# Transposing attention weights: a float32 transpose on TensorE with the split in PSUM, against a float16 split with a transpose by DMA

## The chip, the cores and the metric

The kernel runs on one NeuronCore of a Trainium2 chip. The metric is device time in microseconds, the median of several executions. TensorE, VectorE, ScalarE, GpSimd and SyncE each run their own stream of instructions in order and wait for each other by semaphores. In the rows below they are PE, DVE, ACT, POOL and SP; PEld is TensorE's row of weight loads, which overlap its matmuls. SPq, ACTq are the queues of the engines that issue DMAs.

## What is computed

One inference step of a decoder layer: a prompt of 2048 tokens and eight samples of one token, model width 1024, all in float32. The change lies in the prompt's windowed attention. It is done for mixer A in three dilation branches (window and stride (128,1), (512,4), (2048,16), eight heads of 64) and for mixer B (window 128, eight query and two key heads, sinks). All four are the same banded attention in blocks of 128 queries:

```python
s = jnp.einsum('nbqhgd,nbkhd->nbhgqk', qb, kk, preferred_element_type=jnp.float32) * scale
s = jnp.where(valid[None, :, None, None], s, NEG)
lse = jax.nn.logsumexp(s, axis=-1)
p = jnp.exp(s - lse[..., None])
o = jnp.einsum('nbhgqk,nbkhd->nbqhgd', p.astype(vv.dtype), vv)
```

A block of queries sees its own block of keys and the one before it. Behind the attention come the output projection, cross-attention to 256 memory tokens and a gated feed-forward part with a short convolution.

## The kernel before

Float32 accuracy comes out of split operands: a large product is three matmuls of a high and a low part (`wh`, `wl` of the weights, `h`, `l` of the activations), split by ScalarE (L110, the high part) and VectorE or GpSimd (L120, the rest).

Phase 1 runs the input projection (`gemm_tile`, L667, 24 matmuls of 128x256 for a tile of 128 tokens and 256 columns) over the groups of 512 tokens and the column sets of `ORDER`. It writes q, k and v to DRAM. As soon as a group has its columns, attention jobs are queued: kinds d1, d4 and d16 for the branches of mixer A, b for mixer B, 16 jobs of each kind. Each job is 128 queries and eight heads, and is done as two *quads* of four heads, so there are 128 quads. A quad has one key half (d16, and the first block of the others) or two.

After each tile of the projection `filler` takes a few steps of the attention (`attn_step`, L623). Three steps make one turn, and a turn moves the pipeline by a quad:

- `stage_a` (L534): the scores on TensorE into the banks `se` and `so` (L548); VectorE adds the mask and takes the maximum of each row, one instruction per head (L556), and makes the bias from it (L559); ScalarE takes the exp of each head with its sum (L561). The unnormalised weights are in `sm`, float32, queries on partitions.
- `stage_b` (L565), a turn later: ScalarE copies `sm` to float16 (L569), VectorE subtracts that copy for the second float16 part (L570), both into `p2`; a DMA transpose issued by SyncE (L572) brings `p2` to `pT`, with keys on partitions.
- `stage_c` (L576): for each head and key half five matmuls (L585) with a transposed 128x128 block as the stationary operand, three with the high part and the three bfloat16 parts of the values, two with the low part. A copy (L592) moves the result out of bank `o`.

The queue `ready` (L616, L654) holds two quads between `stage_b` and `stage_c`, so the DMA has two turns. Queries and keys of a job are transposed by TensorE, four 128x128 blocks to a group, into one of two PSUM banks with tag `t` (`t_split` L469 and L473, `t_copy` L478 and L482), and split or copied from there. The buffers: `sm` 2, `p2` 2, `pT` 3, `ost` 5. At the start of the program some of these buffers serve as room for the first tiles of x (`at_start`).

The order in each engine's stream is not the order of the source alone: a scheduler moves instructions by its own timeline, so that pieces of `stage_a` to `stage_c` and transposes stand in the middle of a tile's matmuls. The turn as the source has it is

```python
        elif s == 1:
            nxt = None
            if pipe["b"]:
                jb, i, sm = pipe["b"]
                nxt = (jb, i, *stage_b(jb, i, sm))
```

Phase 2 (output projection, cross-attention, feed-forward) starts when all the attention is done; it uses lines L862 to L864 for its matmuls.

Of the kernel before, what the change touches and what calls it, by code (L numbers as in the profile page):

```python
# [8 lines left out]
F32 = mybir.dt.float32  # L9
F32R = mybir.dt.float32r  # L10
F16 = mybir.dt.float16
BF16 = mybir.dt.bfloat16
ACTF = mybir.ActivationFunctionType
ALU = mybir.AluOpType
# [7 lines left out]
NS = 8  # L22
# [13 lines left out]
def tile_layer(ctx: ExitStack, tc: tile.TileContext, I, C, O):  # L36
    nc = tc.nc
# [32 lines left out]
    act = nc.scalar.activation  # L70
    vec = nc.vector
# [17 lines left out]
    ident = const.tile([128, 128], F32, tag="ident", name="ident")  # L89
# [141 lines left out]
        vec.tensor_scalar(out=out, in0=ss, scalar1=scale, scalar2=EPS, op0=ALU.mult, op1=ALU.add)  # L231
        pl.tensor_tensor(out=out, in0=out, in1=mhalf[:rows, :n], op=ALU.pow)

    # ------------------------------------------------------------------ phase 1
    p1 = ExitStack()
    p1a = ExitStack()
    psA = ctx.enter_context(tc.tile_pool(name="psA", bufs=1, space=PSUM))
# [4 lines left out]
    def bank(tag, bufs, dt=F32):  # L242
        return ps.tile([128, 512], dt, tag=tag, name=tag, bufs=bufs)
# [6 lines left out]
    sinkb = sbR.tile([128, 8], F32, tag="sinkb", name="sinkb")  # L250

    def at_start(tag, bufs):
        """a tile in the place of one that the attention uses later."""
        return sbR.tile([128, 1024], F32, tag=tag, name="x0", bufs=bufs)

    def load_x(src, rows=128, t=None):
# [27 lines left out]
    def xprep(key, nxt=None):  # L284
        rows = NS if key == "s" else 128
        x = x_tiles.pop(key)

        def norm():
            ss = sbL.tile([128, 1], F32, tag="ss", name="ss", bufs=3)
            junk = at_start("sm", 2) if key in range(4) else sbL.tile([128, 1024], F32, tag="xr", name="junk")  # L290
            act(out=junk[:rows], in_=x[:rows], func=ACTF.Square, accum_out=ss[:rows])
            r = sbL.tile([128, 1], F32, tag="r", name="r", bufs=18)
            rms_r(r[:rows], ss[:rows], 1.0 / D, 1, rows)
            rows_r[key] = r

        if key == "s":
            norm()
            pt = bank("t", 2)
            for k in range(8):
                nc.tensor.transpose(pt[:, k * NS:(k + 1) * NS], x[:NS, k * 128:(k + 1) * 128], ident[:NS, :NS])  # L300
            vec.tensor_copy(out=xsT, in_=pt[:, 0:64].rearrange("p (k n) -> p k n", k=8))
            xg = sbL.tile([128, 8, NS], F32, tag="xgs", name="xgs")
            pl.tensor_tensor(out=xg, in0=xsT, in1=vecs[:, 0:8].unsqueeze(2).to_broadcast([128, 8, NS]), op=ALU.mult)
            la = sbL.tile([128, 8, 40], F32R, tag="la", name="la")
            lb = sbL.tile([128, 8, NS], F32R, tag="lb", name="lb")
            pl.memset(la.bitcast(F32), 0.0)
            vec.tensor_copy(out=la[:, :, 0:NS], in_=xg)
            vec.tensor_copy(out=lb, in_=xg)
            lo_of(la[:, :, 32:32 + NS], xg, la[:, :, 0:NS])
            xT[key] = (la, lb)  # L310
            return
        if key != 0:
            norm()
        if key in (1, 2, 3):
            xr = at_start(*(("p2", 2), ("p2", 2), ("pT", 3))[key - 1]).rearrange("p (k t) -> p k t", k=8)
        else:
            xr = sbL.tile([128, 8, 128], F32, tag="xr", name="xr")
        for hf in range(2):
            pt = bank("t", 2)
            for k in range(4):  # L320
                kk = hf * 4 + k
                nc.tensor.transpose(pt[:, k * 128:(k + 1) * 128], x[:, kk * 128:(kk + 1) * 128], ident)
            act(out=xr[:, hf * 4:hf * 4 + 4, :], in_=pt.rearrange("p (k t) -> p k t", k=4), func=ACTF.Copy)
        if key == 0:
            norm()
        xT[key] = xmul(xr, x)
        dma(out=xt_d.rearrange("(k p) t -> p k t", p=128)[:, :, key * 128:(key + 1) * 128], in_=xr)
        rope_tab(key)
        if nxt is not None:
            x_tiles[nxt[0]] = load_x(nxt[1], NS if nxt[0] == "s" else 128)  # L330
# [35 lines left out]
        vec.tensor_tensor(out=out, in0=t1[:rows, :n], in1=t2[:rows, :n], op=ALU.add)  # L366

    def v_split(src, nh):
        """three bf16 parts of the values, exact to float32."""
        v3 = sbL.tile([128, 4, 3, 64], BF16, tag="vs", name="vs", bufs=2)[:, 0:nh]  # L370
        rs = sbL.tile([128, 256], F32, tag="vr", name="vr", bufs=1)[:, 0:nh * 64].rearrange("p (h d) -> p h d", d=64)
        s = src.rearrange("p (h d) -> p h d", d=64)
        pl.tensor_copy(out=v3[:, :, 0, :], in_=s)
        pl.tensor_tensor(out=rs, in0=s, in1=v3[:, :, 0, :], op=ALU.subtract)
        pl.tensor_copy(out=v3[:, :, 1, :], in_=rs)
        pl.tensor_tensor(out=v3[:, :, 2, :], in0=rs, in1=v3[:, :, 1, :], op=ALU.subtract)
        return v3
# [45 lines left out]
            dma(out=s_bk[:, 127, :], in_=z3[:, 0:128])  # L423
            dma(out=s_bv[:, 127, :], in_=z3[:, 128:256])

    # ---- windowed attention, four heads at a time
    class Job:
        def __init__(self, kind, t, c=0):
            self.kind, self.t, self.c = kind, t, c
# [55 lines left out]
    def job_prep(job):  # L485
# [9 lines left out]
        else:  # L495
# [20 lines left out]
            if job.kind == "d4" and job.t > 0:  # L516
                t_split([job.kp[:, 128 * j:128 * j + 128] for j in range(4)], rh[:, 0], rl[:, 0])
                vprev["d4"] = job.vp3
        # halves: list of (slot, v3) in key order
        v3 = job.v3  # L520
        first = job.kind == "d16" or job.t == 0
        if first:
# [11 lines left out]
    def stage_a(job, i):  # L534
# [5 lines left out]
        for ps_i, (a, b) in enumerate(passes):  # L540
            q_ = job.qh if a == 0 else job.ql
            k_ = job.kh if b == 0 else job.kl
            for u in range(2):
                p = 2 * i + u
                pk = 0 if job.kind == "b" else p
                for e in range(2):
                    r = slice(64 * e, 64 * e + 64)
                    mm(S[e][:, u * n:(u + 1) * n], q_[r, p, :], k_[r, s0:s0 + nh, pk, :],  # L548
                       start=(ps_i == 0 and u == 0), stop=(ps_i == len(passes) - 1), skip_group_check=True)
        sm = sbR.tile([128, 4, 256], F32, tag="sm", name="sm", bufs=2)  # L550
        mx = sbR.tile([128, 4], F32, tag="mx", name="mx", bufs=2)
        for u in range(2):
            for e in range(2):
# [9 lines left out]
        return sm  # L563

    def stage_b(job, i, sm):  # L565
        """the weights in two float16 parts, transposed by the DMA."""
        n = 128 * len(job.slots)
        p2 = sbR.tile([128, 2, 4, n], F16, tag="p2", name="p2", bufs=2)
        act(out=p2[:, 0], in_=sm[:, :, 0:n], func=ACTF.Copy)  # L569
        vec.tensor_tensor(out=p2[:, 1], in0=sm[:, :, 0:n], in1=p2[:, 0], op=ALU.subtract)  # L570
        pT = sbR.tile([128, 16, 128], F16, tag="pT", name="pT", bufs=3)[:, 0:n // 16]
        nc.sync.dma_start_transpose(out=pT, in_=p2.rearrange("p g x k -> p (g x k)"))  # L572
        v = pT.rearrange("p (g x h) t -> p g h x t", g=2, x=4)
        return v[:, 0], v[:, 1]

    def stage_c(job, i, ph, pl_):  # L576
        nh = len(job.slots)
# [35 lines left out]
    quads = deque()  # L613
    loaded = deque()
    pipe = {"b": None}
    ready = deque([None] * 2)  # L616
    sub = [0]
    d16_left = [16]

# [3 lines left out]
    def attn_step():  # L623
# [21 lines left out]
# [5 lines that stand above are left out]
            pipe["b"] = pipe["a"]  # L650
            pipe["n"] = nxt
        else:
            ready.append(pipe["n"])
            if len(ready) > 2:  # L654
                e = ready.popleft()
                if e:
                    stage_c(*e)
# [35 lines left out]
    MEM = []  # L693

    def mem_prep(t):
        """a tile of memory tokens, where the keys of the dilated branches have been."""
        if t == 0:
            while any(jb.kind != "b" for jb in [*jobs, *loaded, *(q[0] for q in quads)]):
                filler(1)
# [77 lines left out]
                    jobs.append(Job("b", 4 * b_next + t))  # L777
                b_next += 1

    # ------------------------------------------------------------------ phase 2  # L780
    p1a.close()
    p3 = ExitStack()
    sbA = p3.enter_context(tc.tile_pool(name="sb3a", bufs=1, reuse_waits="tile"))
# [16 lines left out]
    def xtile(nm):  # L800
        return sbA.tile([128, ST], F32, tag="xres", name=nm, bufs=9)[:, 0:NC]

    # state rows of the convolution, features on partitions
    srow = small("srow")[:, 0:384].rearrange("p (a c) -> p a c", a=3)
    sv = I["state_conv"][0].rearrange("n r (f p) -> (n r f) p", p=128)
    dma(out=srow[:, 0:2, :], in_=sv[0:256].rearrange("(a p) c -> p a c", p=128))
# [37 lines left out]
        return [(0, 256), (256, NC)] if has_s else [(0, 512)]  # L844

    def gemm_b(units, panels, pcs, evac, late=None, nm=2, spare=False):
        """units: list of (wh, wl, [panel indices]); evac(m, piece, psum)."""
        P = {}
        nu = len(units)
        for ui, (get, pidx) in enumerate(units):  # L850
# [25 lines left out]
                   lambda m, pi, a, b, p, mp=mp: evac(2 * mp + m, pi, a, b, p), spare=mp == 1 and len(pcs) == 2)  # L876

    class Norm:
        """mean of squares over the features, for each token."""

        def __init__(self, ncol, nlate=0):
            self.nlate, self.ncol, self.sqs, self.n = nlate, ncol, [], 0
# [76 lines left out]
                                     in1=gout[:rows, 512 * i:512 * i + 512], op0=ALU.mult, op1=ALU.mult)  # L959

    def merge(*ts, between=lambda: None):
        """the branches of mixer A weighted by their denominators, both mixers normalised."""
        wide = len(ts) > 1
        nb_ = 4 if wide else 2
        X = [merge_load(t) for t in ts]
# [35 lines left out]
            mo_t[t] = mo  # L1001
            between()

    # ---- decode-step attention over the caches
    def sample_softmax(S, nsl, nh, scale, sink, fix):
        """S: [128, NS, nsl, nh] raw scores -> normalised weights in place."""
        n = NS * nsl * nh
        Sf = S.rearrange("p n g h -> p (n g h)")
        M = sbA.tile([128, 256], F32, tag="sM", name="sM")
# [68 lines left out]
        return go  # L1078

    def pick(n, acc):  # L1080
        """the sum over the partitions, in row n."""
        h, l = (sbA.tile([128, ST], F32R, tag="sm2", name="ah", bufs=7)[:, 0:512] for _ in range(2))
        hi_of(h, acc, "a")
        lo_of(l, acc, h, "v")
        p = bankA("t")
        mm(p[:NS], sel[:, n, :], h, start=True, stop=False)
        mm(p[:NS], sel[:, n, :], l, start=False, stop=True)
        return p
# [60 lines left out]
        sample_steps.append(smp_out(n, "b"))  # L1149
    sample_steps.append(smp_fin)  # L1150

    # ---- cross attention of the samples
    SC = sbA.tile([128, NS, 2, 4], F32, tag="SC", name="SC")

    def xs_begin():
# [48 lines left out]
    cross_steps = [xs_begin] + [xs_score(n) for n in range(NS)] + \  # L1204
        [None] * 2 + soft_steps(SC, 2, 4, 0.0625, None, None) + [xs_out(n) for n in range(NS)] + [xs_fin]

    # ---- one chunk of 512 tokens
    def load_xres(c, hf):
        for m in range(4 * hf, 4 * hf + 4):
            t = xtile("xres")  # L1210
# [7 lines left out]
        return pn  # L1218

    def heads_T(c, oT):  # L1220
        """the merged heads of a chunk, features on partitions."""
        s_in = c == 2

        def one(k):
# [20 lines left out]
    def pre(c, oT, begin):  # L1245
# [20 lines left out]
        gemm_full(oT, pieces(s_in), ev_out)  # L1266
        del oT[:]

        # cross attention, one head after another
        q_t, kv_t, p_t = {}, {}, {}  # L1270
        R = [None]

# [258 lines left out]
        return fin  # L1531

    def fin_steps(c, fin):
        """the last norm and the output, half of the features after the other."""
        last = c == 3
        pts, ys = {}, {}

# [50 lines left out]
                store(i)  # L1588
        return go

    # keys and values of the memory tokens
    def mem_gemm(u, h, l):
        p = bankA("t")
        for kt in range(8):
# [141 lines left out]
```

## Time and profile before

| what | value |
|---|---|
| median of 3 runs | 3255.5 us (3251.39 to 3256.02) |
| span of the profiled execution | 3248.1 us |
| median over the profiled span | 7.4 us (the profiled execution's own time is not listed apart from the three runs) |
| busy share of TensorE, VectorE, ScalarE, GpSimd | 95%, 66%, 44%, 31% |
| attention products, first and last start | 136.6 and 994.9 us |

The span is the time from the first to the last instruction of the profiled execution. Busy time is the time in which an engine has an instruction; a matmul's end is modelled, so the next one often starts before it. An "idle before" with a releaser says who ended an engine's wait. Times in a window count from the span's start.

### The profile page before, as it was taken

The numbers are of one execution on the slowest core, as the hardware profiler recorded it, in microseconds if no ns is written. First come the engines' busy times: TensorE is split into PE (matmuls) and PEld (weight loads), VectorE is DVE, ScalarE is ACT, GpSimd is POOL, SyncE is SP. The second block draws the span as 40 slices with busy tenths as digits, with TensorE's granted clock in tenths as the row PEclk, the third lists the DMA queues.
The fourth block names the chain that finished last, engine by engine and source line by source line (L and its number), as shares of the span: only waits on it lengthen the run. The fifth ranks groups of instructions, "written<-read, shape, count | busy, mean of one in ns | idle before, by whom it ended". The sixth has DMA issues, their size and how long they took to land.

```text
span 3248.1 us, 58089 instructions
## 1 busy us (share of the span) xinstructions
PE 3101.2 (95%) x22280; PEld 2710.7 (83%) x22280; DVE 2140.0 (66%) x4292; ACT 1418.5 (44%) x2795; POOL 1018.7 (31%) x962
## 2 busy tenths in 40 slices
PE   8999989888888999998999999999999999999999
PEld 8888888788877887886887778898877778999998
DVE  7687777887886667664566766555676665654543
ACT  3556654666664444223344333444423333432322
POOL 2611613324343046332204424421454432110102
PEclk9999999999999999999999999999999999999999
DMA  7899998999897346653535545553465535222231
GB/s 210 246 255 241 263 241 231 259 241 216 198 232 225 114 159 212 200 196 130 196 112 174 183 159 175 172 188 111 158 239 213 189 123 185 72 86 92 91 93 66
DMA packets 621838, 580.14 MB, mean 179 GB/s; under 512 B 264141, under 2 KB 554105, under 8 KB 620433
## 3 DMA queue, kind: packets, MB, share of 16 engines
q1 hardware_dynamic: 616808, 572.21, 60.4%
q10 hardware_dynamic: 4608, 4.20, 0.4%
q8 instruction: 175, 2.87, 0.4%
q14 instruction: 103, 0.84, 0.1%
q0 software_dynamic: 144, 0.03, 0.0%
HBM read 457.55 MB, written 136.66 MB: 183 GB/s over the span
## 4 chain that ended last, share of the span: by engine, by line
PE 57%; DVE 5%; DMA 4%; POOL 4%; issue 3%; ACT 2%; SPq 1%; POOLq 0%; DVEq 0%; ACTq 0%
PE g L862 17%; PE g L863 17%; PE g L864 17%; PE s L1337 1%; PE g L1377 1%; DVE wl L120 1%; DMA pT<-p 1%; POOL mrg L990 1%; DMA mrg<-o_d 1%; DMA kx<-in_cache_mem_k_dram 1%; DMA vx<-in_cache_mem_v_dram 1%; POOL kx L1171 1%; ACT wh L110 0%; DMA wr<-in_w_mem_kv_dram 0%; PE t L1360 0%
## 5 line engine op out<-in xcount | busy, mean ns | idle before, releaser
L120 DVE TENSOR_TENSOR wl<-wr,wh 128x1024 fp32r<-128x1024 f32 (+1 forms) x406 | 534.1, 1316 | 369.6 <-ACT wh L110 368.4
L110 ACT ACTIVATE wh<-wr 128x1024 fp32r<-128x1024 f32 (+1 forms) x444 | 460.9, 1040 | 675.5 <-PE g L864 388.2
L862 PE MATMUL g<-h,wh 128*128 128x512 f32 (+2 forms) x2080 | 731.2, 352 | 1.4 <-DVE va L1495 0.7
L863 PE MATMUL g<-h,wl 128*128 128x512 f32 (+2 forms) x2080 | 729.9, 351 | 0.0
L864 PE MATMUL g<-h,wh 128*128 128x512 f32 (+2 forms) x2080 | 726.9, 350 | 0.0
L862 PEld LDWEIGHTS g<-h,wh 128*128 128x128 f32 x2080 | 391.5, 188 | 62.1 <-issue 2.2
L863 PEld LDWEIGHTS g<-h,wl 128*128 128x128 f32 x2080 | 391.5, 188 | 56.0 <-issue 1.7
L864 PEld LDWEIGHTS g<-h,wh 128*128 128x128 f32 x2080 | 391.4, 188 | 55.7
L672 PE MATMUL g<-wh,xh 128*128 128x256 f32 x1152 | 339.9, 295 | 1.9 <-ACT z L383 1.4
L674 PE MATMUL g<-wh,xl 128*128 128x256 f32 x1152 | 332.3, 288 | 0.3 <-DVE xl L120 0.3
L673 PE MATMUL g<-wl,xh 128*128 128x256 f32 x1152 | 331.0, 287 | 0.0
L862 PE MATMUL g<-act,wh 128*128 128x512 f32 (+2 forms) x880 | 311.0, 354 | 15.7 <-ACT act L110 8.0
L863 PE MATMUL g<-act,wl 128*128 128x512 f32 (+2 forms) x880 | 309.7, 352 | 0.0
L864 PE MATMUL g<-act,wh 128*128 128x512 f32 (+2 forms) x880 | 308.6, 351 | 0.0
L561 ACT ACTIVATE sm<-sm,ost 128x256 f32<-128x256 f32 (+1 forms) x512 | 234.7, 460 | 151.7 <-DVE ost L559 151.4
L892 POOL TENSOR_TENSOR sq<-sq 128x512 f32<-128x512 f32 (+1 forms) x83 | 126.2, 1520 | 484.6 <-ACT sq L887 451.8
L672 PEld LDWEIGHTS g<-wh,xh 128*128 128x128 f32 x1152 | 222.8, 193 | 7.2 <-ACT z L383 1.9
L674 PEld LDWEIGHTS g<-wh,xl 128*128 128x128 f32 x1152 | 222.0, 193 | 3.7 <-DVE xl L120 1.0
L673 PEld LDWEIGHTS g<-wl,xh 128*128 128x128 f32 x1152 | 222.7, 193 | 2.0
L862 PE MATMUL g<-oT,wh 128*128 128x512 f32 (+2 forms) x608 | 216.5, 357 | 3.1 <-ACT oT L110 3.1
L863 PE MATMUL g<-oT,wl 128*128 128x512 f32 (+2 forms) x608 | 215.8, 356 | 0.0
L864 PE MATMUL g<-oT,wh 128*128 128x512 f32 (+2 forms) x608 | 211.6, 355 | 0.0
(348 smaller groups left out, 6075.9 us busy)
## 6 DMA issues: line engine op xcount, KB each, us to landing
wr<-in_w_up_dram SPq DMA_DIRECT2D x176, 512.0 KB
wr<-in_w_down_dram SPq DMA_DIRECT2D x80, 512.0 KB
out_dram<-in_cache_a_k_dram SPq DMA_DIRECT2D x32, 1023.5 KB
out_dram<-in_cache_a_v_dram SPq DMA_DIRECT2D x32, 1023.5 KB
wr<-in_w_in_dram SPq DMA_DIRECT2D x60, 512.0 KB
v<-va_d SPq DMA_DIRECT2D x60, 384.0 KB
wr<-in_w_out_dram SPq DMA_DIRECT2D x32, 512.0 KB
wr<-in_w_xq_dram SPq DMA_DIRECT2D x32, 512.0 KB
```

What stands on the lines that cost most here:

```text
L110: act(out=out, in_=in_, func=ACTF.Copy)
L120: e.tensor_tensor(out=out, in0=in_, in1=hi.bitcast(F32), op=ALU.subtract)
L561: act(out=sm[:, x, 0:n], in_=sm[:, x, 0:n], func=ACTF.Exp, scale=0.125, bias=nb[:, x:x + 1], accum_out=job.ost[:, 520 + 4 * i + x:521 + 4 ...
L672: mm(p[:, 0:256], h[:, kt, :], wh[:, q, :], start=(kt == 0), stop=False)
L673: mm(p[:, 0:256], h[:, kt, :], wl[:, q, :], start=False, stop=False)
L674: mm(p[:, 0:256], l[:, kt, :], wh[:, q, :], start=False, stop=(kt == 7))
L862: mm(o, wh[:, q, c], pn[:, 0, a:b], start=st, stop=False)
L863: mm(o, wl[:, q, c], pn[:, 0, a:b], start=False, stop=False)
L864: mm(o, wh[:, q, c], pn[:, 1, a:b], start=False, stop=en)
L892: pl.tensor_tensor(out=acc[:, 0:self.ncol], in0=acc[:, 0:self.ncol], in1=sq[:, 0:self.ncol], op=ALU.add)
L990: pl.tensor_tensor(out=o, in0=o, in1=w[:, g, :].unsqueeze(2).to_broadcast([128, 8, 64]), op=ALU.mult)
L1171: pl.tensor_tensor(out=k[:, 0:1024], in0=k[:, 0:1024], in1=q[:, 0:1024], op=ALU.mult)
```

## The change

`stage_b` no longer splits in SBUF and no longer uses a DMA. For each key half it transposes the four float32 blocks of `sm` on TensorE into a bank `t` (a matmul against the identity, as `t_split` does it), copies the bank to float16 `pT` by ScalarE, and subtracts that copy from the bank by VectorE for the low part. `p2` and the DMA transpose are gone. `sm` has four buffers in place of two. `ready` holds one quad in place of two. `pT` has another shape, and the temporaries at the start that lay in `p2` lie in `sm`. Comments and docstrings are left out. Behind L575 the line numbers of the changed kernel are larger by two.

```diff
@@ xprep
-            junk = at_start("sm", 2) if key in range(4) else sbL.tile([128, 1024], F32, tag="xr", name="junk")
+            junk = at_start("sm", 4) if key in range(4) else sbL.tile([128, 1024], F32, tag="xr", name="junk")
...
-            xr = at_start(*(("p2", 2), ("p2", 2), ("pT", 3))[key - 1]).rearrange("p (k t) -> p k t", k=8)
+            xr = at_start(*(("sm", 4), ("sm", 4), ("pT", 3))[key - 1]).rearrange("p (k t) -> p k t", k=8)
@@ stage_a
-        sm = sbR.tile([128, 4, 256], F32, tag="sm", name="sm", bufs=2)
+        sm = sbR.tile([128, 4, 256], F32, tag="sm", name="sm", bufs=4)
@@ stage_b
-        n = 128 * len(job.slots)
-        p2 = sbR.tile([128, 2, 4, n], F16, tag="p2", name="p2", bufs=2)
-        act(out=p2[:, 0], in_=sm[:, :, 0:n], func=ACTF.Copy)
-        vec.tensor_tensor(out=p2[:, 1], in0=sm[:, :, 0:n], in1=p2[:, 0], op=ALU.subtract)
-        pT = sbR.tile([128, 16, 128], F16, tag="pT", name="pT", bufs=3)[:, 0:n // 16]
-        nc.sync.dma_start_transpose(out=pT, in_=p2.rearrange("p g x k -> p (g x k)"))
-        v = pT.rearrange("p (g x h) t -> p g h x t", g=2, x=4)
-        return v[:, 0], v[:, 1]
+        nh = len(job.slots)
+        pT = sbR.tile([128, 2, 2, 4, 128], F16, tag="pT", name="pT", bufs=3)
+        for hf in range(nh):
+            pt = bank("t", 2)
+            for x in range(4):
+                nc.tensor.transpose(pt[:, x * 128:(x + 1) * 128], sm[:, x, hf * 128:(hf + 1) * 128], ident)
+            v = pt.rearrange("p (x t) -> p x t", x=4)
+            act(out=pT[:, 0, hf], in_=v, func=ACTF.Copy)
+            vec.tensor_tensor(out=pT[:, 1, hf], in0=v, in1=pT[:, 0, hf], op=ALU.subtract)
+        return pT[:, 0], pT[:, 1]
@@
-    ready = deque([None] * 2)
+    ready = deque([None])
@@ attn_step
-            if len(ready) > 2:
+            if len(ready) > 1:
```

The scheduler places the new instructions. Three places in the streams show how. The first is TensorE in the kernel before, in the middle of the d16 jobs; L672 to L674 are the projection's matmuls, L585 the attention's products with a block of `pT` as weights.

```order
L672 MATMUL g_9515<-wh46_8572,xh_9047 128x256
L673 MATMUL g_9515<-wl46_8573,xh_9047 128x256
L674 MATMUL g_9515<-wh46_8572,xl_9048 128x256
L672 MATMUL g_9515<-wh46_8572,xh_9047 128x256
L585 LDWEIGHTS pT_8846
L585 MATMUL o_9055<-v3_8340,pT_8846 128x64
```

Here the products follow a run of the projection's matmuls, in the middle of a tile, and the first weight load is where TensorE stands if `pT` has not landed.

The second is the same engine in the changed kernel, again among the d16 jobs; L548 are the scores of the next quad, L572 the transposes of an earlier quad's weights, L674 to L676 the projection, L587 the products.

```order
L676 MATMUL g_10348<-wh47_9022,xl_9901 128x256
L548 MATMUL se_9829<-kf_9726,qf_9725 128x128
L548 MATMUL so_9830<-kf_9726,qf_9725 128x128
L548 MATMUL se_9829<-kf_9726,qf_9725 128x128
L548 MATMUL so_9830<-kf_9726,qf_9725 128x128
L572 MATMUL t_9847<-ident_81,sm_9714 128x128 x4
L587 LDWEIGHTS pT_9792
L587 MATMUL o_9908<-v3_9278,pT_9792 128x64
```

Between the scores of one quad and the products of another a group of four transposes now stands in TensorE's stream; the products use the `pT` of the group before it.

The third is TensorE in the changed kernel among the b jobs, where no projection is left between the steps; `ringb0` and `ringb1` are the two key halves.

```order
L548 MATMUL so_14249<-ringb0_13451,qh_14117 128x256
L572 MATMUL t_14177<-ident_81,sm_14024 128x128 x4
L572 MATMUL t_14184<-ident_81,sm_14024 128x128 x4
L548 MATMUL se_14248<-ringb1_13452,qh_14117 128x256
L548 MATMUL so_14249<-ringb1_13452,qh_14117 128x256
```

Both groups of a quad (`sm_14024`, into the two `t` banks) now stand inside the score matmuls of the next quad, with no matmul of a projection beside them.

## Rows read from the trace of the kernel before

**Rows 1.** The page, part 1: busy time, share of the span and instructions.

```profile
PE 3101.2 (95%) x22280; PEld 2710.7 (83%) x22280; DVE 2140.0 (66%) x4292; ACT 1418.5 (44%) x2795; POOL 1018.7 (31%) x962
```

**Rows 2.** Busy time by stretch: length, each engine, granted clock, DMA share.

```profile
core 0: us, PE busy (x) PEld busy (x) DVE busy (x) ACT busy (x) POOL busy (x), PEclk, DMA share, GB/s
100.00:300.00 200.00, 189.27 (x2128) 178.72 (x2127) 162.19 (x474) 117.45 (x310) 57.97 (x63) 0.99 0.99 252
850.00:1005.00 155.00, 126.30 (x1610) 113.17 (x1610) 122.81 (x348) 98.62 (x266) 67.09 (x44) 0.92 1.00 237
0.00:1005.00 1005.00, 895.20 (x10315) 828.52 (x10316) 779.25 (x2298) 580.49 (x1557) 345.97 (x324) 0.96 0.97 237
1005.00:3248.00 2243.00, 2205.97 (x11968) 1882.18 (x11966) 1360.72 (x1994) 838.00 (x1238) 672.68 (x638) 0.99 0.45 152
```

**Rows 3.** TensorE's waits, whole span: us in total, times, longest.

```profile
PE o L585 <- DMA pT<-p: 48.7, 37, 3.1
...
PE se L548 <- DVE mx L556: 14.4, 15, 2.5
...
PE t L473 <- DVE ql L120: 4.3, 4, 2.5
...
PEld L585 <- DMA pT<-p: 58.2, 44, 3.3
```

**Rows 4.** The products' line L585: duration min/median/max in ns, starts, forms.

```profile
L585 PE MATMUL o<-v,pT x3000: 192/193/261, 136.6 to 788.3; 128*128 128x64 bf16 x188
L585 PE MATMUL o<-v3b,pT x1240: 193/193/258, 790.0 to 994.9; 128*128 128x64 bf16 x178
```

**Rows 5.** Timeline of TensorE from 612.67 us: start, us, what.

```profile
612.67 0.28 PE L672 MATMUL g<-wh,xh 128*128 128x256 f32 x1
612.79 0.28 PE L673 MATMUL g<-wl,xh 128*128 128x256 f32 x1
612.91 0.28 PE L674 MATMUL g<-wh,xl 128*128 128x256 f32 x1
613.03 0.60 PE L482 MATMUL t<-ident,raw 128*128 128x128 f32 x4
613.38 0.36 PE L672 MATMUL g<-wh,xh 128*128 128x256 f32 x1
613.59 0.28 PE L673 MATMUL g<-wl,xh 128*128 128x256 f32 x1
```

**Rows 6.** The transposes of line L482: duration min/median/max in ns.

```profile
L482 PE MATMUL t<-ident,raw x160: 270/273/477, 116.3 to 647.0; 128*128 128x128 f32 x160
```

**Rows 7.** Groups by form, VectorE and ScalarE: busy us, mean ns, idle before.

```profile
L570 DVE TENSOR_TENSOR p<-sm,p 128x1024 f16<-128x1024 f32 x84 | 120.3, 1432 | 34.9 <-ACT p L569 34.6
L569 ACT ACTIVATE p<-sm 128x1024 f16<-128x1024 f32 x84 | 88.3, 1052 | 37.4 <-DMA pT<-p 36.8
L570 DVE TENSOR_TENSOR p<-sm,p 128x512 f16<-128x512 f32 x44 | 38.6, 878 | 24.1 <-ACT p L569 23.9
L120 DVE TENSOR_TENSOR ql<-t,qh 128x512 fp32r<-128x512 f32 x44 | 30.0, 681 | 2.1 <-ACT qh L110 2.1
L569 ACT ACTIVATE p<-sm 128x512 f16<-128x512 f32 x44 | 27.6, 627 | 22.5 <-DMA pT<-p 21.8
L110 ACT ACTIVATE qh<-t 128x512 fp32r<-128x512 f32 x44 | 25.9, 588 | 19.6 <-PE t L473 13.7 <-PE o L585 4.2 <-PE so L548 1.7
```

**Rows 8.** The DMA transposes in SP's queue: min/median/max in ns.

```profile
L572 SPq DMA_TRANSPOSE pT<-p x128: 1231/2986/7377, 129.0 to 986.7; - x128
```

**Rows 9.** Groups by form of `stage_a`: busy us, mean ns.

```profile
L561 ACT ACTIVATE sm<-sm,ost 128x256 f32<-128x256 f32 x336 | 166.4, 497 | 104.2 <-DVE ost L559 104.0
...
L561 ACT ACTIVATION_READ_ACCUMULATOR sm<-sm,ost 128x1 f32 x512 | 96.1, 188 | 0.0
...
L556 DVE CUSTOM_DVE_ANT_0 sm<-se,mask 128x256 f32<-128x256 f32 x168 | 64.7, 417 | 6.9 <-PE so L548 3.0 <-PE se L548 2.9
...
L559 DVE TENSOR_SCALAR ost<-mx 128x4 f32<-128x4 f32 x128 | 42.2, 330 | 0.8
```

**Rows 10.** Line L473, q/k transposes, by stretch: TensorE matmul, weight loads, clock.

```profile
100.00:300.00 200.00, 13.31 (x92) 10.03 (x92) 0.99 0.99 252
```

## The prediction

> **What bounds the kernel now.** I read the page's busy shares first: TensorE is busy for 95% of the span [rows 1], no other engine comes near. Then the stretches: the attention runs from about 100 to 1005 us, and behind it 2243 us follow in which TensorE is busy for 2206 [rows 2]. The change touches nothing behind 1005 us, so the question is what the first 1005 us become. There TensorE is busy for 895 us, VectorE for 779, ScalarE for 580, and the DMA engines are full (share 0.97); the mean granted clock is 0.96 [rows 2]. The clock has two levels, 1.2 and 2.4 GHz, so a mean of 0.96 is some 80 us at the lower one, which loses 40 us of matmul work.
>
> Third, who keeps TensorE waiting. One wait stands out: the attention's products (`stage_c`, L585) for the transposed weights `pT` that the DMA brings, 48.7 us in 37 waits on the matmul row, and 58.2 us in 44 on the row of weight loads, where the reader should look, because a wait shorter than a matmul's modelled tail shows only there [rows 3]. The other waits for VectorE are small: 14.4 us of the scores for the mask step, 4.3 us of the q/k transposes for the split that frees their bank [rows 3]. So the transposes by DMA cost TensorE 58 us directly, and more by the clock: in the stretch from 100 to 300 us, with little idle time, the clock is 0.99, in the last one, from 850 to 1005 us, with 29 us idle, it is 0.92 [rows 2].
>
> **The change part by part.** *Added on TensorE.* `stage_c` runs five products for each transposed 128x128 block, and there are 3000 + 1240 of them [rows 4], so there are 4240 / 5 = 848 blocks, in 212 groups of four, one group for each key half of each quad. The trace has the same operation already: four float32 transposes against `ident` (L482). Between the big matmul at 612.91 and the second one behind the group, at 613.59, lie 0.68 us; two matmuls without a group between them start 0.24 us apart. A group costs 0.44 us, changes of operand included [rows 5]. 212 x 0.44 = **+93 us**. They stand in TensorE's own stream, which is the path, so nothing hides them but a wait that they fill.
>
> *The duration of one transpose* is 273 ns [rows 6], two and a half times the 0.11 us spacing: they overlap in the pipeline. The Trainium skill (VectorE: DVE Perf Modes, the three transpose paths and the rules for kernel authors) advises TensorE for a 128x128 transpose where PSUM will do, at 390 ns against 1309 ns by DMA; by its figures, one block after the other, the 848 blocks would be an estimated gain of 848 x 0.919 = 779 us. The trace disagrees with the 390 (it has 273), and with the use of the difference: what counts is on whose time a transpose runs, and the DMA's ran beside TensorE and held it for 58 us. The sum stands on the 0.44 us.
>
> *Removed.* The wait for the DMA goes: **-58 us**, if nothing takes its place. Of the 40 us that the low clock takes, between nothing and all may come back. I take half, **-20 us**: the pT waits are the largest group in that part but not the only one, and new waits (below) keep some of it.
>
> *VectorE and ScalarE.* VectorE subtracts two 128x512 pieces out of PSUM in place of one 128x1024 out of SBUF. The before rows come to 120.3 + 38.6 = 158.9 us; 212 pieces at the 0.681 us of the q split are 144.4, so 14.5 us less. ScalarE: 88.3 + 27.6 = 115.9 us against 212 x 0.588 = 124.7, so 9 us more [rows 7]. At 779 and 580 busy of 1005 us neither sets the pace, so I cost both at nothing; if VectorE were the bound these would be a small gain.
>
> *SP's queue and the DMA engines.* 128 transposes leave SP's queue, at a median of 2.99 us each [rows 8]. Loads queued behind them go out earlier. TensorE hardly waits for those loads, so I count no gain.
>
> *Added waits.* Three things are new: a group of transposes waits for the exps of its quad (ScalarE), it waits for one of the two `t` banks, which the q/k transposes share and which VectorE's subtraction frees, and the products wait for that subtraction. From scores to the last exp a two-half quad takes 4 x 0.417 + 0.330 + 4 x (0.497 + 0.188) = 4.7 us [rows 9]; transposed, copied and subtracted takes 0.44 + 0.588 + 0.681 = 1.7 us more. In the stretches with big matmuls a turn of the pipeline has 17 to 30 of them (0.12 us each) beside the attention's own work, and most of both is covered. In the last stretch several turns have none, and scores, transposes and products follow each other directly, as the third piece of the order shows: what stands behind a waiting transpose there is everything, because TensorE's stream is in order. The bounds: three kinds at 4.3 us, as the q/k transposes wait now, is 13 us; three at 14.4 us, as the scores wait for VectorE now, is 43 us. I take the middle, **+28 us**. That `ready` holds one quad less costs nothing beyond this.
>
> *Sum.* 93 - 58 - 20 + 28 = **+43 us**. The profiled execution's span is 3248.1 us, so it becomes 3291; the median of the runs is 3255.5, 7.4 us over that span, so **3298.5 us**. With the bounds (clock -40 to 0, waits 13 to 43) the sum runs from +8 to +78 us, 3263.5 to 3333.5.
>
> **The rivals.** A difference of 0.2%, 6.5 us, is about what a measurement of this kernel can tell from no change.
>
> *Faster.* The 93 us fill waits. Besides the 58 and the whole 40, the 14.4 and 4.3 us of waiting for VectorE vanish, because more TensorE work stands between producer and consumer, and the new waits stay at nothing: 93 - 58 - 40 - 19 = -24 us, **3231.5**. For it: ScalarE's copy also stalled on `p` being read by the DMA, and this delayed exps. Against it: from 100 to 300 us the clock is 0.99 and TensorE is idle for 11 of 200 us [rows 2], so the groups there have nothing to fill. It turns faster where more than 100 of the 117 us are recovered. Chance 0.12.
>
> *Even.* All of the wait and of the clock's 40 us come back, and the new waits are a few us to the bound of 13: 93 - 98 + 5 = 0 us, **3255.5**. Chance 0.12.
>
> *The `t` banks become the bound.* A bank is held for 1.7 us by a group, of which 1.27 us are ScalarE and VectorE; there are two banks for the 212 new groups and for the q/k transposes. If in the 84 two-half quads (the wide form) [rows 7] the next user waits half of the 1.27 us, that is 84 x 0.63 = 53 us on top: +96, **3351.5**. For it: VectorE serves in order and the mask step of four 0.417 us pieces can stand ahead. Against it: the present waits on that ring are 4.3 us. Chance 0.14.
>
> *The clock falls more often.* If a group of transposes breaks up the run of matmuls as an idle gap does, the lower clock gets none of its 40 us back and takes half as much again: 93 - 58 + 20 + 28 = +83, **3338.5**. Against it: the q/k transposes are in the present stream too, 92 of them from 100 to 300 us [rows 10], where the clock is 0.99 [rows 2]. Chance 0.10. The Trainium skill (TensorE: Matmul & The Clock Gate, Part 4) says that transposes do not count as TensorE being busy for the clock; by that rule this rival gains weight. No row here separates the two.
>
> That the change does not do what it says can be left out: the order shows the 848 transposes on TensorE and none on SP's queue.
>
> **How the numbers follow.** The forecast has 0.52. Slower by over 0.2% are the forecast, the bank and the clock: 0.52 + 0.14 + 0.10 = 0.76. The even case gives 0.12 to within 0.2%, and the first rival 0.12 to faster. The forecast's own range is 3263 to 3334. To leave out no more than 2 in 10 it is widened to **3240 to 3350**: downwards over the even case and into the faster one, upwards over the clock's rival and up to the bank's price.
>
> **What would show it.** Right: 848 more matmuls on TensorE's row, spaced by 0.11 us in fours; no wait of the products for a DMA; the attention ends some 43 us later than 1005 us, and the stretch behind it keeps its 2243 us. The new waits appear on TensorE as transposes waiting for `sm` of ScalarE and products waiting for `pT` of VectorE, in sum 13 to 43 us, mostly behind 700 us; the clock up to the end of the attention is about 0.98. Wrong: groups much dearer or cheaper than 0.44 us, waits for the `t` bank of over 50 us, a clock at or under 0.96, or a part of the 2243 us that moves.

## The result, and the profile of the changed kernel

The change makes the kernel slower: 3290.8 us (median of four runs, 3286.08 to 3294.24) against 3254.2 us (four runs, 3251.39 to 3256.02), **+36.6 us**, a ratio of 1.0114 with a 95% interval of 1.0099 to 1.0129. The forecast was +43 us, 3298.5 us, and "slower" had 0.76. The profiled execution of the changed kernel has a span of 3292.5 us, 44.4 us over the one before and at the upper end of its runs, so its rows show about 8 us more than the medians do.

Part 1 of the page answers to [rows 1]: TensorE has 848 matmuls more and 96.7 us more of busy time, VectorE and ScalarE are where they were.

```profile
PE 3197.9 (97%) x23128; PEld 2801.3 (85%) x23128; DVE 2137.8 (65%) x4376; ACT 1427.3 (43%) x2879; POOL 979.1 (30%) x962
```

The windows of the changed kernel, columns as in [rows 2]. The attention ends 40 to 45 us later, so its windows reach to 1045 us.

```profile
100.00:300.00 200.00, 194.48 (x2137) 184.44 (x2136) 148.77 (x453) 108.64 (x294) 56.07 (x64) 0.99 0.65 202
850.00:1045.00 195.00, 177.67 (x2258) 160.38 (x2256) 149.90 (x480) 131.44 (x384) 61.81 (x50) 0.96 0.43 136
0.00:1045.00 1045.00, 989.56 (x11170) 918.09 (x11171) 780.40 (x2382) 588.74 (x1640) 309.75 (x324) 0.98 0.58 175
1045.00:3292.00 2247.00, 2208.37 (x11960) 1883.26 (x11958) 1357.43 (x1994) 838.59 (x1239) 669.35 (x638) 0.99 0.45 152
```

Read the third row against the third of [rows 2]. TensorE's busy time grows by 94.4 us (989.56 less 895.20), its idle time falls from 109.8 to 55.4 us, and the difference, 40 us, is what the stretch grew by. The DMA engines go from a share of 0.97 to 0.58, and the granted clock from 0.96 to 0.98. The fourth row shows that the 2243 us behind are 2247, and the 4 us between them are a matter of where the window's edge lies: the time is lost in the attention.

The products' line, as in [rows 4], tells the same without a window's edge: its last start moves from 994.9 to 1039.0 us, 44.1 us of the span's 44.4.

```profile
L587 PE MATMUL o<-v,pT x3000: 192/193/277, 128.4 to 832.2; 128*128 128x64 bf16 x188
L587 PE MATMUL o<-v3b,pT x1240: 191/193/261, 836.1 to 1039.0; 128*128 128x64 bf16 x178
```

TensorE's waits in the changed kernel, whole span, answering to [rows 3] (us in total, times, longest):

```profile
PE se L548 <- DVE mx L556: 6.1, 5, 2.5
PE t L572 <- DVE ql L120: 4.8, 5, 1.7
PE t L572 <- DVE pT L575: 4.6, 6, 1.6
PE o L587 <- ACT pT L574: 4.2, 7, 1.5
PE t L473 <- DVE pT L575: 3.5, 4, 1.5
...
PE t L572 <- ACT xr L323: 2.3, 2, 1.5
...
PE t L572 <- DVE ringb L120: 0.9, 2, 0.6
...
PE t L572 <- ACT sm L561: 0.7, 1, 0.7
```

No wait of the products for a DMA is left. In its place stand small ones, 21.0 us in all without the first row: 16.1 us are for a `t` bank that an earlier user holds (the rows of L572 that end with `ql`, `pT`, `xr` or `ringb`, and L473's for `pT`), 4.2 us are products that wait for ScalarE's copy, and only 0.7 us are transposes that wait for the exps (2.1 us on the row of weight loads). The scores' wait for the mask step fell from 14.4 to 6.1 us without being touched by the change.

The new instructions by form, and the transposes' line (duration min/median/max):

```profile
L575 DVE TENSOR_TENSOR pT<-t,pT 128x512 f16<-128x512 f32 x212 | 144.2, 684 | 43.3 <-ACT pT L574 42.3
L574 ACT ACTIVATE pT<-t 128x512 f16<-128x512 f32 x212 | 122.6, 590 | 122.9 <-PE t L572 121.7
```
```profile
L572 PE MATMUL t<-ident,sm x848: 270/273/477, 123.2 to 1036.4; 128*128 128x128 f32 x170
```

These match the prediction's 212 groups, 144.4 us, 124.7 us and 273 ns. Two groups in the timeline, start and length first: four transposes behind scores at 641.79 with the next matmul at 642.29, and four between two products.

```profile
641.79 0.66 PE L572 MATMUL t<-ident,sm 128*128 128x128 f32 x4
642.29 0.25 PE L587 MATMUL o<-v,pT 128*128 128x64 bf16 x3
...
300.80 0.40 PE L587 MATMUL o<-v,pT 128*128 128x64 bf16 x8
301.03 0.64 PE L572 MATMUL t<-ident,sm 128*128 128x128 f32 x4
301.50 0.22 PE L587 MATMUL o<-v,pT 128*128 128x64 bf16 x2
```

Products start 0.03 us apart, so the last of the eight starts at 301.00, and the next behind the group 0.50 us later: this group adds 0.47 us.

### The profile page after: what moved, and what is told of

Its sections match the earlier page's. It is cut to its first block, busy times and chain, and to the rows that moved or that the text cites. A ratio compares the mean times of both kernels' runs of the same rounds, so it can differ in the third digit from the quotient of the medians.

```text
span 3292.5 us, 59690 instructions
## 1 busy us (share of the span) xinstructions
PE 3197.9 (97%) x23128; PEld 2801.3 (85%) x23128; DVE 2137.8 (65%) x4376; ACT 1427.3 (43%) x2879; POOL 979.1 (30%) x962
## 4 chain that ended last, share of the span: by engine, by line
PE 59%; DVE 3%; POOL 2%; DMA 2%; issue 2%; ACT 1%; SPq 0%; POOLq 0%; DVEq 0%; ACTq 0%
PE g L864 18%; PE g L865 18%; PE g L866 18%; PE s L1339 1%; PE g L1379 1%; DVE wl L120 1%; POOL mrg L992 0%; DMA mrg<-o_d 0%; PE t L1362 0%; DMA vx<-in_cache_mem_v_dram 0%; PE t L1543 0%; PE t L1230 0%; POOL vx L1185 0%; DVE cv L1462 0%; PE t L903 0%
## 5 line engine op out<-in xcount | busy, mean ns | idle before, releaser
L674 PE MATMUL g<-wh,xh 128*128 128x256 f32 x1152 | 337.2, 293 | 2.2 <-DVE xh L114 1.6
L676 PE MATMUL g<-wh,xl 128*128 128x256 f32 x1152 | 333.7, 290 | 0.5 <-DVE xl L120 0.5
L674 PEld LDWEIGHTS g<-wh,xh 128*128 128x128 f32 x1152 | 220.8, 192 | 5.9 <-issue 1.7
L676 PEld LDWEIGHTS g<-wh,xl 128*128 128x128 f32 x1152 | 220.6, 191 | 2.2 <-DVE xl L120 1.0
L864 PE MATMUL g<-oT,wh 128*128 128x512 f32 (+2 forms) x608 | 215.4, 355 | 1.7 <-ACT oT L110 1.7
L120 POOL TENSOR_TENSOR wl<-wr,wh 128x1024 fp32r<-128x1024 f32 x38 | 93.0, 2447 | 410.1 <-ACT wh L110 410.1
```

The costliest lines, as they stand in the source:

```text
L120: e.tensor_tensor(out=out, in0=in_, in1=hi.bitcast(F32), op=ALU.subtract)
L674: mm(p[:, 0:256], h[:, kt, :], wh[:, q, :], start=(kt == 0), stop=False)
L676: mm(p[:, 0:256], l[:, kt, :], wh[:, q, :], start=False, stop=(kt == 7))
L864: mm(o, wh[:, q, c], pn[:, 0, a:b], start=st, stop=False)
```

## The experiments

The theory from the prediction: the transposes cost TensorE their full spacing, and take away a wait that was worth less. The rivals for what the trace shows: the time is lost to the new waits or the shorter queue `ready`, to the clock, or the old wait was a matter of a queue or a buffer that could have been mended without any of this. Every ratio is to the kernel before, measured again beside each round, with its 95% interval.

**The DMA transposes taken out of the kernel before.** The products use the untransposed parts.

```diff
-        p2 = sbR.tile([128, 2, 4, n], F16, tag="p2", name="p2", bufs=2)
+        p2 = sbR.tile([128, 2, 4, n], F16, tag="p2", name="p2", bufs=5)
...
-        nc.sync.dma_start_transpose(out=pT, in_=p2.rearrange("p g x k -> p (g x k)"))
-        v = pT.rearrange("p (g x h) t -> p g h x t", g=2, x=4)
+        v = p2.rearrange("p g x (h t) -> p g h x t", t=128)
```

> The kernel before without its DMA transposes: the products take the split weights as they stand, queries on partitions, so the attention's results are left wrong; everything else is kept (the float16 split on ScalarE and VectorE, two quads in ready). Path theory (what the DMA transposes cost is the wait of the products, 58 us, and a part of the 36 to 40 us of low clock): 60 to 95 us less than before, 3160 to 3195 us. Rival, that the transposes also slow the kernel by filling the DMA engines and SP's queue: clearly more than that, under 3150 us. Rival, that the products' waits would move to another producer: 3220 to 3255 us.

Measured: 3176.5 us, 0.9762 (0.9737 to 0.9787), **-78 us**. The window to the end of its attention:

```profile
0.00:925.00 925.00, 874.38 (x10306) 816.36 (x10307) 780.43 (x2298) 576.69 (x1557) 341.42 (x324) 0.98 0.65 196
```

The wait for `pT` is gone, the scores still wait 13.4 us for the mask step. So the DMA transposes cost TensorE 78 us in all: 58 as its wait and 20 besides, clock included. With the rest of the kernel kept, this is what another way of transposing can win at most.

**The TensorE transposes taken out of the changed kernel**, copy and subtraction kept, from `sm`.

```diff
-            pt = bank("t", 2)
-            for x in range(4):
-                nc.tensor.transpose(pt[:, x * 128:(x + 1) * 128], sm[:, x, hf * 128:(hf + 1) * 128], ident)
-            v = pt.rearrange("p (x t) -> p x t", x=4)
+            v = sm[:, :, hf * 128:(hf + 1) * 128]
```

> The changed kernel without the transposes on TensorE: ScalarE's copy and VectorE's subtraction read the weights from SBUF in the same 212 pieces, not from a bank, so the weights are not transposed and the attention's results are left wrong. Path theory (848 transposes at 0.11 us stand on the path): 93 us less than the changed kernel, 3190 to 3205 us. Rival, that the loss comes from the shorter queue of quads, the shared t banks or the split in pieces: much of it stays, 3230 to 3270 us.

Measured: 3186.3 us, 0.9783 (0.9762 to 0.9804), 4 us under the range. The transposes with their bank, and with the split that reads it, cost 104.5 us (3290.8 less 3186.3). The page:

```profile
PE 3085.9 (97%) x22280; PEld 2699.7 (85%) x22280; DVE 2155.5 (68%) x4376; ACT 1423.6 (45%) x2879; POOL 1003.6 (32%) x962
```

TensorE is idle for 98.6 us of this span (3184.5 less 3085.9) and for 94.6 us of the changed kernel's (3292.5 less 3197.9). So the cost is time in which TensorE is busy: the transposes fill hardly more waiting than they make. Both ablations end within 10 us of each other, so what this run keeps of the change (212 pieces, four `sm` buffers, one quad less in `ready`) comes to about that in sum.

**Every transpose of the changed kernel done twice**, into the same place.

```diff
                 nc.tensor.transpose(pt[:, x * 128:(x + 1) * 128], sm[:, x, hf * 128:(hf + 1) * 128], ident)
+                nc.tensor.transpose(pt[:, x * 128:(x + 1) * 128], sm[:, x, hf * 128:(hf + 1) * 128], ident)
```

> The changed kernel with each of the 848 transposes done twice into the same place of the bank. Path theory: another 93 us, 3375 to 3395 us. Rival, that TensorE still has idle time that such work fills: under 3340 us.

Measured: 3349.2 us, 1.029 (1.0265 to 1.0314), 58.4 us over the changed kernel, not 93, and between the two ranges. The spacing is not the reason. The timeline of one doubled group, where L572 and L573 are the two transposes:

```profile
640.43 0.27 PE L572 MATMUL t<-ident,sm 128*128 128x128 f32 x1
640.54 0.27 PE L573 MATMUL t<-ident,sm 128*128 128x128 f32 x1
640.64 0.27 PE L572 MATMUL t<-ident,sm 128*128 128x128 f32 x1
640.75 0.27 PE L573 MATMUL t<-ident,sm 128*128 128x128 f32 x1
```

They start 0.11 us apart as before. The window and the products' last start show where some of the rest went:

```profile
L588 PE MATMUL o<-v3b,pT x1240: 191/193/261, 879.2 to 1092.8; 128*128 128x64 bf16 x178
...
0.00:1095.00 1095.00, 1049.69 (x11999) 987.12 (x12000) 777.88 (x2382) 590.35 (x1640) 308.80 (x324) 0.99 0.55 166
```

The attention ends 53.8 us later than the changed kernel's (1092.8 less 1039.0), 39 less than 93. TensorE is idle for 45.3 us here against 55.4, 10 us less, and the clock is up again. In the record of the granted clock up to the end of the attention 48 us are at the lower level in the changed kernel and 14 here: 34 us fewer, in which half of the work is lost, so 17 us. That is 27 of the 39 us; the other 12 I can't place, and these rows are of one execution each (the run with one quad more in `ready`, below, has the transposes once and 31 us at the lower level). What decides about the clock is the mean over each of the four runs: 0.991 to 0.994 here, 0.987 to 0.990 in the changed kernel, 0.978 to 0.986 in 61 runs of the kernel before. Twice as many transposes went with a higher clock, not a lower one.

**One quad more in `ready` of the changed kernel**, as many as before the change.

```diff
-    ready = deque([None])
+    ready = deque([None] * 2)
...
-            if len(ready) > 1:
+            if len(ready) > 2:
```

> The changed kernel with two quads in ready between transposing and the products, as before the change, in place of one. Path theory: the products' waits for the split are about 5 to 10 us in all, so between 3280 us and no change (3294). Rival, that the shorter queue made the loss: back to 3255 to 3265 us.

Measured: 3286.5 us, 1.01 (1.0076 to 1.0124), 4 us under the changed kernel and inside its spread. The shorter queue costs next to nothing.

**The depth of `ready` in the kernel before.** With three quads the DMA gets a turn more; the fourth `pT` buffer takes the room of the second `qh`, `ql` and `qf`, so a control has that alone (`bufs=1` for the three). With one quad it gets a turn less.

```diff
-    ready = deque([None] * 2)
+    ready = deque([None] * 3)
...
-            if len(ready) > 2:
+            if len(ready) > 3:
```

> The kernel before with three quads in ready and four pT buffers in place of two and three, so a DMA transpose has a turn more; the room comes from one buffer of qh and ql each in place of two. Path theory with the wait as latency: most of the products' 58 us of waiting goes and some of the low clock, 3185 to 3225 us, below both kernels. Rival, that the DMA engines, full in that part, are a matter of throughput and a deeper queue only waits later: 3245 to 3262 us.

> The kernel before with one quad in ready, as the changed kernel has it, DMA transposes kept. If the wait is latency against the turns in ready, it grows by a good part of a turn for many of the 128 quads: 3300 to 3400 us, and the shorter queue is one that only the change to TensorE makes possible. Rival, throughput: 3245 to 3270 us.

> Control for the run with three in ready: the kernel before with one buffer of qh and ql each and nothing else changed. Under every theory 3250 to 3265 us.

Measured: three quads 3271.8 us, 1.0051 (1.0034 to 1.0069); one quad 3277.8 us, 1.0075 (1.0053 to 1.0097); the control 3256.9 us, 1.001 (0.9994 to 1.0025). Three quads were expected to gain, and lose 15 us against their control, above both ranges; one quad lies between its two. TensorE's waits with three and the window of its attention, then the waits of the control, then with one:

```profile
PE o L585 <- DMA pT<-p: 44.2, 31, 6.7
PE se L548 <- DVE mx L556: 23.0, 16, 4.1
...
0.00:1023.00 1023.00, 912.86 (x10298) 845.48 (x10299) 785.43 (x2298) 578.01 (x1556) 338.79 (x324) 0.94 0.96 232
```
```profile
PE o L585 <- DMA pT<-p: 60.1, 40, 4.1
PE se L548 <- DVE mx L556: 4.8, 8, 1.7
```
```profile
PE o L585 <- DMA pT<-p: 92.2, 60, 5.1
```

With one quad the wait nearly doubles over [rows 3]. With three it falls by 16 us against the control (60.1 to 44.2), the longest single one grows from 4.1 to 6.7, and the scores' wait for the mask step grows by 18, from 4.8 to 23.0; the clock falls to 0.94. The DMA share is 0.96 in this run: a turn more in the queue didn't free the DMA engines, and the wait moved. The depth of two was the best of the three. The control also says how far a wait of one execution carries: it takes 0.1% more time than the kernel before, with an interval that includes no difference, and has 60.1 and 4.8 us in rows that read 48.7 and 14.4 there.

**Three `p2` buffers in the kernel before**, in the room of the same q tiles, because ScalarE waits for `p2` until the transposes have read it.

```diff
-        p2 = sbR.tile([128, 2, 4, n], F16, tag="p2", name="p2", bufs=2)
+        p2 = sbR.tile([128, 2, 4, n], F16, tag="p2", name="p2", bufs=3)
```

> The control with one buffer of qh and ql, and three buffers of p2 in place of two, DMA transposes and two quads in ready kept. If the products wait because ScalarE's copy is held by the two p2 buffers (it waits 31 us for them in the control, 58 us in the kernel before), the waits shrink: 3225 to 3245 us. If the DMA engines, full in that part, are the limit: 3250 to 3265 us, as the control (3257).

Measured: 3261.7 us, 1.0032 (1.0013 to 1.0051), 4.8 us over the control, with intervals that overlap. TensorE still waits 54.0 us in 42 waits for `pT`, against 60.1 in 40, though ScalarE's own wait for the buffer, 31.1 us in the control, is gone. That buffer isn't what holds the transposes back.

**Half by each way.** If the DMA engines are what is full, and each group on TensorE costs 0.44 us, then taking some of the transposes from the DMA should do better than all or none. Here the second key half of the 84 two-half quads goes by TensorE, the first half and the one-half quads by DMA (`sm` has three buffers, `ready` two quads).

```diff
+        mixed = nh == 2
+        nd = 1 if mixed else nh
...
+        p2 = sbR.tile([128, 2, 4, nd * 128], F16, tag="p2", name="p2", bufs=2)
+        act(out=p2[:, 0], in_=sm[:, :, 0:nd * 128], func=ACTF.Copy)
+        vec.tensor_tensor(out=p2[:, 1], in0=sm[:, :, 0:nd * 128], in1=p2[:, 0], op=ALU.subtract)
...
+        nc.sync.dma_start_transpose(out=pD, in_=p2.rearrange("p g x k -> p (g x k)"))
...
+        for x in range(4):
+            nc.tensor.transpose(pt[:, x * 128:(x + 1) * 128], sm[:, x, 128:256], ident)
+        z = pt.rearrange("p (x t) -> p x t", x=4)
+        act(out=pe[:, 0], in_=z, func=ACTF.Copy)
+        vec.tensor_tensor(out=pe[:, 1], in0=z, in1=pe[:, 0], op=ALU.subtract)
```

> The kernel before, but of each of the 84 quads with two key halves the second half goes by TensorE as in the change (84 groups at 0.44 us, 37 us) and the first by the DMA; two quads in ready, three buffers of sm, p2 of half the size. If a full set of DMA engines makes the products wait, transposes of half the size shorten it: 37 us more, 40 to 50 us of waiting and some 15 us of low clock less, 3225 to 3250 us. If the waits stay as they are: 3275 to 3295 us.

Measured: 3241.8 us, **0.9961 (0.9947 to 0.9976)**, 13.5 us under the kernel before: this beats both kernels. Its window, and its waits for `pT` on both of TensorE's rows:

```profile
0.00:990.00 990.00, 927.25 (x10641) 860.60 (x10642) 784.88 (x2382) 585.69 (x1640) 326.04 (x324) 0.98 0.85 217
```
```profile
PE o L596 <- DMA pT<-p: 15.1, 16, 2.2
...
PEld L596 <- DMA pT<-p: 19.6, 20, 2.4
```

At the prediction's price 84 groups cost 84 x 0.44 = 37 us. The wait falls from 58.2 to 19.6 us, 39 less; the DMA share falls from 0.97 to 0.85. The clock is at 0.98, as in the changed kernel, which got it with 212 groups (by the runs: a mean of 0.987 over ten, against 0.9885). So 84 groups take back two thirds of the wait and nearly as much of the clock as 212 did. The third `sm` buffer was not tested alone; the next run has two and still gains, so it isn't the whole of it.

**Two other splits.** One leaves the early quads to the DMA: only mixer B, branch d1 from its ninth block and d4 from its third group of 512 tokens are mixed, 62 quads, with `sm` as in the kernel before. The other adds the second quad of each one-half job to the 84, 22 groups more.

```diff
-        mixed = nh == 2
+        mixed = nh == 2 and (job.kind == "b" or (job.kind == "d1" and job.t >= 8) or (job.kind == "d4" and job.t >= 2))
```
```diff
+        if nh == 1 and i == 1:
+            pt = bank("t", 2)
+            for x in range(4):
+                nc.tensor.transpose(pt[:, x * 128:(x + 1) * 128], sm[:, x, 0:128], ident)
```

> The same mixture for 62 of the 84 quads alone: all of kind b, and those of d1 and d4 in the later half of the prompt, since the DMA waits lie there (1.4 us from 100 to 300 us, 47 behind); 27 us of transposes; sm and p2 as in the kernel before. If the waits go as in the run before: 3215 to 3245 us, below both kernels. If not: 3265 to 3285 us.

> The mixture of the run h1 with the second quad of each one-half job (22 groups, 10 us) by TensorE as well, since the DMA engines are still full from 500 to 700 us there, where these jobs lie. If the remaining waits of the products (15 to 20 us) go with the fullness: 3230 to 3242 us, a little below h1 (3241.8). If 10 us of transposes buy less than that: 3243 to 3252 us.

Measured: 62 quads 3249.0 us, 0.9984 (0.9971 to 0.9997); 84 quads and 22 groups 3245.3 us, 0.9978 (0.9965 to 0.9991). The first lies between the two ranges that were expected, the second in the one for no further gain: neither is better than the plain half. Among these three splits the gain is flat, 0.2 to 0.4%.

## Why the prediction was right

**The price on TensorE held in the main.** 212 groups at 0.44 us were +93; taking them out gave 104.5. The 0.44 was read from one group among the projection's matmuls; between two products, the commonest place, a group adds 0.47 us, and 212 x 0.47 is 100. The price is full only where nothing is left to fill or to come back: the second set of transposes cost 58.4. The prediction's remark that the trace disagrees with 390 ns compares unlike things: that figure of the Trainium skill (VectorE: DVE Perf Modes, the three transpose paths) is for a bfloat16 block, and the 273 ns are for a float32 one.

**The wait went, as costed.** -58 came from the row of weight loads, and no wait of the products for a DMA is left. The ablation of the DMA transposes gave -78, the wait and 20 us more, which is also what the prediction had with its clock (-58 - 20). Reading the matmul row alone (48.7) would have been 10 us short.

**The clock's return came out as forecast, partly by luck.** The prediction took 40 us as lost and half of it as coming back; the half was a choice between nothing and all. The runs bear it out: a mean clock of 0.982 over 61 runs of the kernel before loses 59 us, 0.9885 over the four of the changed kernel loses 38, so **21 us** come back (24 in the ablation, at 0.989). The two profiled executions show less:

```profile
core 0: 3248.1 us, clock 0.984
core 0: 3292.5 us, clock 0.987
```

They are a run of the kernel before with a clock above its mean and the lowest of the changed kernel's four. By their record of the granted clock 72 us are at the lower level up to 1005 us before and 48 up to 1045 after: half of the 24 us between them, 12 us, came back in this pair.

**The new waits were mis-sized a little, and their kind was in part wrong.** They are 21 us, inside the 13 to 43 and under the 28, and 16.6 of them lie behind 700 us, as forecast. But the prediction's signs named transposes waiting for the exps, and these are 0.7 us. Most are for the `t` bank, 16.1 us, a wait that it had counted as one of three and not named among the signs. The products wait for ScalarE's copy (4.2 us) and hardly for VectorE's subtraction (0.3). That the order of the stream covers the exps, and that nothing covers a bank with several users, is how I read it; no run shows it.

**Two falls were not in the sum.** The scores' wait for the mask step fell by 8.3 us, and the 4.3 us in which the q/k transposes waited for the split of `ql` went (the 4.8 us of L572 for `ql` took their place, and are in the 21). Whether the first is the change's doing is open: the control with one buffer each of `qh`, `ql` and `qf` has 4.8 us in that row with all its DMA transposes.

With the measured sizes and the profiled pair's clock the sum is 100 - 58 - 12 + 21 - 8 - 4 = **+39 us**, against 44 by the profiled spans; with the runs' clock, -21, it is **+30 us**, against 36.6 by the medians. Some 5 to 7 us stay unplaced. The errors of the first sum (7 too little for the groups, 7 too much wait, 12 not counted) partly cancelled; its +43 is closer than its terms.

**The rivals.** *Faster* and *even* needed 93 us or more of filled waits; the most there was to win is 78, by the ablation. *The `t` banks* did become the largest new wait, with 16.1 us and not the 53 that would have made them the bound. *The clock falls more often* is refuted by the granted clock, in the attention 0.96 before, 0.98 after, 0.99 with twice the transposes, and in the same order in the runs. The Trainium skill (TensorE: Matmul & The Clock Gate, Part 4) says that transposes do not count in the same way as TensorE being busy for the clock; the trace doesn't bear this out for these float32 transposes, since more of them went with more of the higher level. Whether that is because they count, or because they stand where TensorE would else have waited, no run here separates.

**What stays open.** That the DMA's wait comes from full DMA engines rests on the share (0.97 with the wait, 0.96 where a deeper queue didn't help, 0.85 with a third of it) and on what failed (queue depth, `p2` buffers). No run changed the share by other traffic alone, so it is supported, not shown. A rival is SyncE's queue, in which a transpose takes a median of 2.99 us before [rows 8] and 1.25 us in the half split, whose DMA transposes are smaller:

```profile
L574 SPq DMA_TRANSPOSE pT<-p x128: 1231/1251/3392, 130.1 to 974.1; - x128
```

No run separates the two. Nor is it settled why three quads in `ready` are slower than two.

## What to carry to other kernels

Work that moves onto the bounding engine costs its spacing in that engine's stream, and gains only the wait that it takes away and what the clock gives back: look for that row first (the one of weight loads too) and compare the numbers. Read the spacing beside the instructions where the work will stand, and the clock over several runs, not from one profile. Where each of two ways is limited by another resource, split the work between them before choosing: 84 groups of 212 took back most of the wait, and this beat both pure versions, the one by DMA by 0.4%. Here, with the DMA engines at a share of 0.96, a longer queue or another buffer moved the wait, and didn't shorten the time.

## What the runs showed of the hardware that was not expected

The same 848 transposes cost 104.5 us when added to none and 58.4 us when added a second time, at the same spacing of 0.11 us. The second time went with a higher clock (0.991 to 0.994 by the runs, against 0.987 to 0.990) and 10 us less idle time on TensorE, so part of the added work paid for itself. And the DMA transposes weigh on the DMA engines beyond their bytes. The page's lines on DMA, before and after:

```profile
DMA packets 621838, 580.14 MB, mean 179 GB/s; under 512 B 264141, under 2 KB 554105, under 8 KB 620433
DMA packets 400659, 524.65 MB, mean 159 GB/s; under 512 B 42956, under 2 KB 332920, under 8 KB 399248
```

That is 10% fewer bytes and 36% fewer packets in the whole program, and all the packets that went are of under 512 B. In the attention alone the bytes fall by 23% (237 GB/s over 1005 us to 175 over 1045), and the DMA engines' busy time by 38% (0.97 of 1005 us to 0.58 of 1045).
